# A planned decoder kernel: rotary tables first, the first head's projections moved forward, new durations and an exclusion rule in the plan

## The chip, the core and the metric

The kernel runs on one core of one Trainium2 chip. The time is that of one execution on the device in microseconds (us). The engines are PE (TensorE, matrix products), V (VectorE, "DVE" in the profile), A (ScalarE, "ACT"), G (GpSimd, "POOL") and the queue of SyncE, "SP", which issues most loads. PE, V, A and G each work through their own instructions in program order; semaphores hold an instruction until what it reads is there. "Half clock" is TensorE at 1.2 GHz instead of 2.4 GHz, 0.50 in the profile's granted clock.

## The reference

Two decoder layers on 512 tokens of width 1024, in float32:

```python
h = rms_norm(x, attn_pre_g[l]);  proj = h @ w_in[l]
qa, ka, va, qb, kb, vb, f_logit = jnp.split(proj, split_at, axis=-1)
qa = partial_rotary(...); ka = partial_rotary(...)      # first 16 of each 64 columns
oa = diff_attention(qa, ka, va, lam)                    # 4 heads, softmax 1 - lam * softmax 2
oa = rms_norm(oa, diff_sub_g[l]) * (1.0 - lam_init)
log_f = jax.nn.log_sigmoid(f_logit + forget_bias[l])
ob = forgetting_attention(qb, kb, vb, log_f)            # 8 heads, a decay added to the logits
x = x + rms_norm(concat([oa, ob]) @ w_out[l], attn_post_g[l])
h = rms_norm(x, ffn_pre_g[l])
x = x + rms_norm((silu(h @ w_gate[l]) * (h @ w_up[l])) @ w_down[l], ffn_post_g[l])
```

The cosines and sines of the rotary step come from `positions`, 512 integers.

## The kernel before

Tokens and features lie in tiles of 128 partitions by 512 columns. Every operand of a large product is split into a high part `h` (a rounded copy made by A) and a low part `l` (the rest, a subtraction by V or G), and each product is three matmuls: high by high, high by low, low by high. A weight chunk is so loaded by SP into a raw buffer (`wr`, two of them), copied by A (`wh`) and subtracted by V or G (`wl`).

A layer has these stages. **Values of the differential heads** (`va`): four banks of PSUM, one per block of 128 tokens, 24 matmuls each in four chunks. **Attention**: for each differential head a projection of k and q (`pj_kd`, `pj_qd`, 24 matmuls each), the rotary step (V: product with `cosT`, a shuffle, product with `sinT`; G: the sum), the split into `ksd` and `qsd`; then for each of four blocks of queries the scores (`sd`), their minimum on V, the exponential on A, a reciprocal on V, a scaling on G, the combination of both softmaxes on V (`ed`), the transposes on PE (`ptd`), their split on A and V, and the product with the values (`od`), normed through a further product (`ss`). The forgetting heads (`pj_kf`, `pj_qf`, `sf`, `ptf`, `of`) get their bias `ae` from G, and after the exponential a reciprocal and a scaling of `ae` on V; their values are `vb`. **Output projection** (`o`), whose weights partly use own buffers (`wo1h`, `wo1l`), then the **FFN** (`pj_g`, `pj_u`, `d`). Layer 0 begins with the loads, the norm (`h_a`), transposes (`hp_a`) and splits of `hT`.

In the attention stages the order on every engine is written by a planner. Each step is an `Op` with an engine, a duration, what it depends on, the buffers that it takes and gives, and a key; `Plan.run` keeps a clock per engine, starts the step that can start first (the lowest key among those ready), and emits the instruction. Steps of PE with the key `FILLER` (projections, `vb`, `o`) fill PE where no score, transpose or value product is ready. The planned times vanish; the order stays, and the instructions then wait for each other by semaphores alone. What the planner takes for durations are lines such as

```python
def dV(n):
    return 68 + 1.04 * n
```

in ns for n columns (`dA`, `dG` for A and G). Layer 0's beginning is planned too (`start`, `tables`). `START` sets the order of the loads. Rotary tables: SP loads the positions as eight blocks of 16 x 32, V works out the angles (`rot`), A takes sines and cosines, and the result goes to DRAM and back into `cosT` and `sinT`. The raw value weights lie in the later `mixd` and `rawv` tiles.

Of the kernel before, what the change touches and what calls it, by code (L numbers as in the profile page):

```python
# [11 lines left out]
F32 = mybir.dt.float32  # L12
F32R = mybir.dt.float32r
# [4 lines left out]
P = 128  # L18
S = 512
# [15 lines left out]
TB = S // 16  # L35
VA_C, VA_T = 4, 1
# [7 lines left out]
C_ID, C_M, C_F, NKEEP, C_U = 0, 128, 640, 641, 641  # L44
NCONST = 1153
# [15 lines left out]
class Op:  # L61
    def __init__(self, eng, dur, fn, deps, key, take, give, lat):
        self.eng, self.dur, self.fn, self.key, self.take, self.give, self.lat = eng, dur, fn, key, take, give, lat
        self.users, self.after, self.left, self.ready, self.end = [], [], 0, 0.0, None
        for d in deps:
            d.users.append(self)
            self.left += 1


class Plan:  # L70


    def __init__(self, slots, margin):
        self.free = {k: [0.0] * n for k, n in slots.items()}
        self.margin, self.ops, self.last, self.idle = margin, [], {}, None

    def add(self, eng, dur, fn, deps=(), key=0.0, take=(), give=(), lat=0.0, order="", ready=0.0):
        o = Op(eng, dur, fn, deps, key, take, give, lat)
# [18 lines left out]
    def run(self, pin, first):  # L97
        clock = dict.fromkeys("VAGQ", 0.0)
        clock["P"] = first
        cands = {e: [o for o in self.ops if o.eng == e and not o.left] for e in clock}  # L100
        todo = len(self.ops)
        while todo:
            best = None
            for e, c in cands.items():
                opts = []
                for o in c:
                    s = self.slots_at(o)
                    if s is not None:
                        r = max(s, o.ready)
                        opts.append((max(r, clock[e]), o.key, r, o))  # L110
# [12 lines left out]
            clock[o.eng] = start + o.dur  # L123
            o.end = start + o.dur + o.lat
# [34 lines left out]
def _constants():  # L159
# [6 lines left out]
    c[:, C_M + S - P:C_M + S] = np.where(r[None, :] > r[:, None], np.float32(-BIG), np.float32(0.0))  # L166
    expo = np.arange(0, ROT, 2, dtype=np.float32) / np.float32(ROT)
    inv_freq = (np.float32(1.0) / np.power(np.float32(500000.0), expo).astype(np.float32)).astype(np.float32)
    c[:, C_F] = inv_freq[r // 16]
    return c  # L170
# [3 lines left out]
def hymba_block(ctx, tc, x_d, pos_d, apre_d, win_d, fb_d, lq1_d, lk1_d, lq2_d, lk2_d, dsg_d, wout_d, apost_d,  # L174
# [64 lines left out]
    V.memset(sinT, 0.0)  # L239
    G.memset(cosT, 1.0)  # L240
# [102 lines left out]
    for l in range(DEPTH):  # L343
        win = win_d[l]
        with ExitStack() as actx:
# [12 lines left out]
            mixed_d = ap.tile([P, NDIFF, S], F32, name=f"mixd{l}", tag="v8", bufs=5)  # L358
            if l == 0:
                raw_v = ap.tile([P, NDIFF, S], F32, name=f"rawv{l}", tag="v8", bufs=5)  # L360
# [18 lines left out]
            vd, tab = [], []  # L379
# [12 lines left out]

            def start():

                plan.free.update(g=[], v8=[0.0], qs=[], ks=[])
# [9 lines left out]
                idd = dma(con[:, :P], con_d[:, :P], P)  # L405

                def w_load(c):
                    raw = (mixed_d, raw_v)[c // 2][:, 2 * (c % 2):2 * (c % 2) + 2]
                    if c == 0:
                        dst = q_tile("wva0h"), q_tile("wva0l")  # L410
                    elif c < 3:
                        w = k_tile(f"wva{c}")
                        dst = w[:, 0], w[:, 1]
                    else:
                        dst = [wpool.tile([P, WCH], F32R, name=f"{x}_va3", tag=x).rearrange("p (a b) -> p a b", a=2)
                               for x in ("wh", "wl")]
                    hi, lo = dst
                    d = dma(raw, win[2 * c * P:(2 * c + 2) * P, VA:VA + S].rearrange("(k p) n -> p k n", p=P), 2 * S)
                    ops = []
                    for k in range(2):  # L420
                        wva[2 * c + k] = hi[:, k], lo[:, k]
                        a = add("A", dA(S), lambda k=k: A.copy(hi[:, k], raw[:, k]), [d], key=-85 + c,
                                take=["w"] if c == 3 and k == 0 else [], order="hi w" if c == 3 and k == 0 else "")
# [13 lines left out]
                zeros = sinT.bitcast(mybir.dt.bfloat16)  # L437
# [16 lines left out]
                for t in range(NT):  # L454
# [24 lines left out]
                    for z in range(2):  # L479
# [20 lines left out]
                        p = add("P", 436, tr, [v, idd], key=key, take=["ts"[z]], give=["e"])  # L500
# [3 lines left out]
                for t in range(NT):  # L504
                    for c in range(4):
                        def vas(t=t, c=c):
                            if t == NT - 1:
# [4 lines left out]
                                         key=500 + VA_C * c + VA_T * t)  # L512
                    vd_split(t, [done[t, 3]])
                for c in range(4):
                    add("P", 0, lambda: None, [done[t, c] for t in range(NT)], key=-99,
                        give=(["qs", "qs"], ["ks"], ["ks"], ["w"])[c])
                add("P", 0, lambda: None, wl[2] + wl[3], key=-99, give=["v8"])
                add("P", 0, first_va.clear, [done[t, 0] for t in range(NT)], key=-99)
                return hT[NT - 1, 1]

            def tables(last):

# [3 lines left out]
                tab_d = dpool.tile([4, 8, S], F32, name="tab_d", tag="tabd")  # L526
# [4 lines left out]
                def get(dst, src, n, **kw):  # L531
                    return add("Q", max(400, 1.43 * n), lambda: nc.sync.dma_start(dst(), src), key=1, lat=2000,
                               order="ld" + "".join(f" {k}" for k in kw.get("take", ())), **kw)

                def positions():
                    w = rbuf("rd", F32, "rot")
                    x["p"] = w[:, :TB].bitcast(I32)
                    x["a"], x["n"] = w[:, TB:2 * TB], w[:, 2 * TB:3 * TB]
                    x["t"] = w[:, 4 * TB:8 * TB].rearrange("p (x j) -> p x j", x=4)
                    blocks = pos_d[0].rearrange("(b j) -> b j", j=TB)  # L540
                    return [lambda f=f: nc.sync.dma_start(x["p"][16 * f:16 * f + 16], blocks) for f in range(8)]

                def sums():
                    x["tu"] = rbuf("rc", F32, "tu")
                    return x["tu"]
                dp = add("Q", 3000, positions, key=1, lat=2000, order="ld rd", take=["rd"])
                dc = get(lambda: con[:, P:], con_d[:, P:NKEEP], S)
                du = get(sums, con_d[:, C_U:C_U + S], S, take=["rc"])

                v = op("V", 100, lambda: V.tensor_copy(x["a"], x["p"]), [dp])  # L550
                v = op("V", 100, lambda: V.tensor_scalar_mul(x["a"], x["a"], con[:, C_F:C_F + 1]), [v, dc])
                for sc in (2.0 ** 22, 2.0 ** 11, 1.0):
                    v = op("V", 100, lambda sc=sc: V.tensor_scalar(
                        x["n"], x["a"], scalar1=1.0 / (2.0 * math.pi * sc), scalar2=MAGIC, op0=ALU.mult,
                        op1=ALU.add), [v])
                    v = op("V", 100, lambda: V.tensor_scalar(x["n"], x["n"], scalar1=-MAGIC, scalar2=1.0, op0=ALU.add,
                                                             op1=ALU.mult), [v])
                    for part in _two_pi_parts():
                        v = op("V", 110, lambda sc=sc, part=part: V.scalar_tensor_tensor(
                            x["a"], x["n"], -part * sc, x["a"], op0=ALU.mult, op1=ALU.add), [v])  # L560
                v = op("V", 100, lambda: V.tensor_scalar(x["a"], x["a"], scalar1=3.1415925, scalar2=-3.1415925,
                                                         op0=ALU.min, op1=ALU.max), [v])
                v = op("V", 110, lambda: V.scalar_tensor_tensor(x["n"], x["a"], -1.0, x["a"], op0=ALU.mult,
                                                                op1=ALU.max), [v])
                a = op("A", 1500, lambda: A.activation(x["t"][:, 3], x["a"], AF.Sin), [v] + last)
                c = [op("A", 220, lambda j=j: A.activation(x["t"][:, j], x["n"], AF.Sin, bias=halfpi, scale=-1.0), [a])
                     for j in range(2)]
                v = op("V", 100, lambda: V.tensor_scalar_mul(x["t"][:, 2], x["t"][:, 3], -1.0), [a])
                p = op("A", 1300, lambda: A.preload_act_table_set("natural_log_exp_and_others"), c)
                d = op("Q", 500, lambda: nc.sync.dma_start(tab_d.rearrange("x f (b j) -> (f b) x j", j=TB), x["t"]),  # L570
                       [v, *c], lat=2000, give=["rd"])
                rows = tab_d.rearrange("x f s -> (x f) s")
                for T, r0 in ((cosT, 0), (sinT, ROT)):
                    for m in (0, HD):
                        tab.append(op("Q", 400, lambda T=T, r0=r0, m=m: nc.sync.dma_start(
                            T[m:m + ROT], rows[r0:r0 + ROT]), [d], lat=2000))
# [48 lines left out]
            def load(src, shape, name, eng=G, dst=None, take=("w",)):  # L625
# [17 lines left out]
                def lo():  # L643
# [5 lines left out]
                                give=["wr"])  # L649
# [3 lines left out]
            def fillers(pieces, deps, take={}, give=()):  # L653
# [679 lines left out]
```

## Time and profile before

| | |
|---|---|
| three runs, median | 1262.27 us (1256.56 to 1264.68) |
| the profiled execution | 1261.95 us, its span 1260.1 us |
| PE busy | 1223.8 us (97%) |
| V, A, G busy | 633.0, 520.8, 279.6 us |

The span is what the trace covers; the execution takes 1.85 us more. A matmul's end is modelled and overlaps the next one's start, so that PE looks busy while it is refilled; its idle time is what the windows leave over, and is a lower bound of what it loses.

### The profile page before, as it was taken

Reading aid. Unit: us, or ns where it says so; the run is one execution under the profiler, and the core shown is the slowest. Engines: PE = TensorE matmul, PEld = TensorE weight load, DVE = VectorE, ACT = ScalarE, POOL = GpSimd, SP = SyncE. Lnnn points to the kernel's source line nnn. Section 1 sums busy time; section 2 is a strip of 40 time slices with the busy share of each in tenths; the row PEclk is TensorE's granted clock in tenths of the full one; section 3 lists DMA queues with packets and bytes.
Section 4 is the critical chain, followed back from the end, with each engine's and each line's share of the span. In section 5 each row is a group of like instructions: output and inputs, shape, how many; then the busy total and the mean of one; then the engine's idle time right before and its main releaser. Section 6 shows DMA issues by size and latency. Waiting matters only on the chain.

```text
span 1260.1 us, 15914 instructions
## 1 busy us (share of the span) xinstructions
PE 1223.8 (97%) x5949; PEld 1015.2 (81%) x5949; DVE 633.0 (50%) x1188; ACT 520.8 (41%) x1008; POOL 279.6 (22%) x318
## 2 busy tenths in 40 slices
PE   8999999999999999999999999999999999999998
PEld 5788877798888888888877878777988888888886
DVE  7597858563333333222556867685633333332224
ACT  5465757453222222222344647674522222222221
POOL 1555557220000000000246535671100000000001
PEclk9999999999999999999999999999999999999999
DMA  7334343404333334223413333442133333332222
GB/s 241 79 84 111 93 117 103 132 18 117 98 89 98 101 101 131 88 99 106 128 35 93 88 98 93 125 129 81 51 101 100 91 93 101 100 118 87 97 100 84
DMA packets 158717, 125.94 MB, mean 100 GB/s; under 512 B 7008, under 2 KB 134112, under 8 KB 158640
## 3 DMA queue, kind: packets, MB, share of 16 engines
q1 hardware_dynamic: 158496, 124.40, 33.3%
q8 instruction: 47, 0.77, 0.3%
q10 hardware_dynamic: 144, 0.52, 0.1%
q14 instruction: 30, 0.25, 0.1%
HBM read 114.32 MB, written 2.20 MB: 92 GB/s over the span
## 4 chain that ended last, share of the span: by engine, by line
PE 56%; issue 31%; DVE 6%; ACT 3%; POOL 2%; DMA 1%; SPq 0%; POOLq 0%; DVEq 0%; ACTq 0%
PE pj_g L204 10%; PE pj_u L204 10%; PE d L204 9%; PE o L204 4%; PE pj_kd L204 3%; PE pj_qd L204 3%; PE vb L204 3%; PE va L204 3%; PE pj_kf L204 2%; PE pj_qf L204 2%; PE sd L204 2%; PE sf L204 1%; PE ptf L209 1%; PE of L204 1%; DVE ae L1033 1%
## 5 line engine op out<-in xcount | busy, mean ns | idle before, releaser
L204 PE MATMUL pj_g<-hT_h,wh_g 128*128 128x512 f32 (+1 forms) x384 | 142.9, 372 | 0.0
L204 PE MATMUL pj_g<-hT_h,wl_g 128*128 128x512 f32 (+1 forms) x384 | 142.6, 371 | 0.0
L204 PE MATMUL pj_g<-hT_l,wh_g 128*128 128x512 f32 (+1 forms) x384 | 142.6, 371 | 0.0
L204 PE MATMUL pj_u<-hT_h,wh_u 128*128 128x512 f32 (+1 forms) x368 | 140.1, 381 | 0.0
L204 PE MATMUL pj_u<-hT_l,wh_u 128*128 128x512 f32 (+1 forms) x368 | 139.8, 380 | 0.0
L204 PE MATMUL pj_u<-hT_h,wl_u 128*128 128x512 f32 (+1 forms) x368 | 139.8, 380 | 0.0
L204 PE MATMUL d<-wh_d,hh 128*128 128x512 f32 x336 | 130.8, 389 | 0.0
L204 PE MATMUL d<-wl_d,hh 128*128 128x512 f32 x336 | 130.7, 389 | 0.0
L204 PE MATMUL d<-wh_d,hl 128*128 128x512 f32 x336 | 130.7, 389 | 0.0
L258 DVE TENSOR_TENSOR wl_u<-wr_u,wh_u 128x1024 fp32r<-128x1024 f32 x44 | 53.9, 1225 | 150.2 <-ACT wh_u L257 150.2
L258 DVE TENSOR_TENSOR wl_d<-wr_d,wh_d 128x1024 fp32r<-128x1024 f32 x42 | 51.4, 1224 | 146.9 <-ACT wh_d L257 146.5
L257 ACT CAST wh_u<-wr_u 128x1024 fp32r<-128x1024 f32 x44 | 46.3, 1052 | 157.9 <-PE pj_g L204 151.6
L257 ACT CAST wh_d<-wr_d 128x1024 fp32r<-128x1024 f32 x42 | 44.3, 1054 | 157.3 <-PE d L204 134.3
L257 ACT CAST wh_g<-wr_g 128x1024 fp32r<-128x1024 f32 x44 | 46.3, 1053 | 145.8 <-issue 124.7
L1206 DVE TENSOR_TENSOR sg<-pj_u,sg 128x512 f32<-128x512 f32 x44 | 30.4, 692 | 141.7 <-PE pj_u L204 141.7
L270 POOL TENSOR_SCALAR v_fp<-s_fp 128x1 f32<-128x1 f32 x8 | 4.0, 506 | 367.0 <-ACT junk L276 366.7
L204 PEld LDWEIGHTS pj_g<-hT_h,wl_g 128*128 128x128 f32 x384 | 72.4, 188 | 12.6
L204 PEld LDWEIGHTS pj_g<-hT_l,wh_g 128*128 128x128 f32 x384 | 72.3, 188 | 12.5
L204 PEld LDWEIGHTS pj_g<-hT_h,wh_g 128*128 128x128 f32 x384 | 72.3, 188 | 12.4
L204 PEld LDWEIGHTS pj_u<-hT_h,wh_u 128*128 128x128 f32 x368 | 69.3, 188 | 13.1
L204 PEld LDWEIGHTS pj_u<-hT_h,wl_u 128*128 128x128 f32 x368 | 69.1, 188 | 13.1
L204 PEld LDWEIGHTS pj_u<-hT_l,wh_u 128*128 128x128 f32 x368 | 69.2, 188 | 12.9
(272 smaller groups left out, 2768.8 us busy)
## 6 DMA issues: line engine op xcount, KB each, us to landing
wr_g<-in_w_gate_dram SPq DMA_DIRECT2D x44, 512.0 KB, 3.8
wr_u<-in_w_up_dram SPq DMA_DIRECT2D x44, 512.0 KB, 3.8
wr_d<-in_w_down_dram SPq DMA_DIRECT2D x44, 512.0 KB, 3.4
wr_o<-in_w_out_dram SPq DMA_DIRECT2D x16, 512.0 KB, 4.2
wr_kd<-in_w_in_dram SPq DMA_DIRECT2D x8, 512.0 KB, 4.0
wr_qd<-in_w_in_dram SPq DMA_DIRECT2D x8, 512.0 KB, 4.0
ksd<-ksd SPq DMA_DIRECT2D x16, 256.0 KB, 2.9
wr_kf<-in_w_in_dram SPq DMA_DIRECT2D x8, 512.0 KB, 3.8
```

The costliest lines, as they stand in the source:

```text
L204: ins = PE.matmul(out, a, b, start=start, stop=stop)
L209: ins = PE.transpose(out, a, idn)
L257: A.copy(hi, raw)
L258: (eng or V).tensor_sub(lo, raw, hi.bitcast(F32))
L270: G.tensor_scalar(v, s2[:, 0:1], scalar1=s2[:, 1:2], scalar2=EPS, op0=ALU.add, op1=ALU.add)
L1033: return V.tensor_scalar_mul(b["e"][:, :n], b["e"][:, :n], b["l"])
L1206: V.tensor_mul(sg, pu, sg)
```

## The change

1. The rotary tables are made at the very beginning (`rotary`): A loads its trigonometric table first, then issues the gain and then the positions, one load of 128 x 4 single integers; V works on 128 x 32; A writes sines and cosines into two tiles; PE transposes these and A copies them to `cosT` and `sinT`. The way through DRAM is gone.
2. The raw value weights go into `pt` buffers, their halves into tiles of the `v8` pool, and `mixed_d` of layer 0 is made later.
3. The value matmuls of tokens 256 to 511 get a key near that of fillers, and the first head's k and q projections of layer 0 a lower one than theirs.
4. Durations in the plan grow (`dV`, `dA`, `dG`, scores, exponentials, norms).
5. A step on V marked `port` starts in the plan only after the last such step of G, and any step of G only after the last marked one of V. This is in the planner; no instruction gets a new wait from it.

```diff
-VA_C, VA_T = 4, 1
+VA_C, VA_T, VA_EARLY = 4, 1, 2
...
+        self.port = port or eng == "G"
...
                         r = max(s, o.ready)
+                        if o.port:
+                            r = max(r, port["G" if e == "V" else "V"])
...
+            if o.port:
+                port[o.eng] = start + o.dur
...
             def dV(n):
-                return 68 + 1.04 * n
+                return 110 + 1.05 * n
             def dA(n):
-                return 60 + 0.83 * n
+                return 115 + 0.83 * n
             def dG(n):
-                return 120 + 2.15 * n
+                return 180 + 2.17 * n
...
+                tc.keep_in_program_order(A.preload_act_table_set("trig_and_small"))
                 g0 = gpool.tile([P, D], F32, name="g_apre0", tag="gain")
...
+                rotary()
...
                         done[t, c] = add("P", 1390, vas, hT[t, c // 2] + wl[c] + ([done[t, c - 1]] if c else []),
-                                         key=500 + VA_C * c + VA_T * t)
+                                         key=(500 if t < VA_EARLY else FILLER - 20) + VA_C * c + VA_T * t)
...
+            def rotary():
+                key = -95
...
+                v = op("A", 500, lambda: A.dma_start(pos, pos_d[0].rearrange("(j p) -> p j", p=P)), [], lat=3000)
+                v = op("V", 80, lambda: V.tensor_copy(pf, pos), [v])
+                v = op("V", 700, lambda: [lambda f=f, c=c: V.tensor_scalar_mul(an[:, f * NT:(f + 1) * NT], pf, c)
+                                          for f, c in enumerate(_inv_freq())], [v])
...
+                for z, dep in ((0, v2), (1, v)):
+                    a = op("A", 800, lambda z=z: [place(z, half, m) for half in range(2) for m in range(2)], [dep])
+                    def tr(z=z):
+                        x[z] = (bank_t, bank_s)[z](f"rot{z}")
+                        for j in range(NT):
+                            transpose(x[z][:, j * P:(j + 1) * P], tabs[z][:, j * P:(j + 1) * P], ident)
+                    p = op("P", 436, tr, [a, idd[0]], take=["ts"[z]])
+                    ends.append(op("A", dA(S), lambda z=z: A.copy((cosT, sinT)[z], x[z]), [p], give=["ts"[z]]))
+                add("A", 0, lambda: None, ends, key=-99, give=["rc", "rc", "rd"])
...
+                du = add("Q", 1.43 * S, sums, key=1, lat=2000, order="ld rc", take=["rc"])
...
-                last_tile[:] = fillers([(650, piece(k)) for k in range(KT)], [ready], take={0: ["g"]}, give=["w"])
+                last_tile[:] = fillers([(650, piece(k)) for k in range(KT)], [ready], take={0: ["g"]}, give=["w"],
+                                       key=FILLER - 40 if kind == "d" and l == z == 0 else FILLER)
...
-                v = add("V", dV(n), top, [o], key=n_key, give=["s"])
-                return b, add("A", 282 + 0.83 * n, expo, [v], key=n_key)
+                v = add("V", dV(n)+80, top, [o], key=n_key, give=["s"])
+                return b, add("A", 370 + 0.87 * n, expo, [v], key=n_key)
...
-                    v = add("V", 75, inv, [a], key=nk)
-                    v = add("V", 70 + 0.65 * n, norm, [v], key=nk)
+                    v = add("V", 110, inv, [a], key=nk)
+                    v = add("V", 185 + 0.5 * n, norm, [v], key=nk, port=True)
```

Marked `port` in the same way: V's weight splits, the rotary product with `sinT`, the splits of `ksd` and `qsd`, the combination `ed`, the split before `ss` and the last scaling of `mixd`.

**First place: V at the beginning of layer 0.** `xs` are the tokens, `h_a` the normed ones, `rot` the angles, `hp_a` the transposed ones. Before:

```order
L468 ISA ss_a_116 128x1
L483 SCALAR_TENSOR_TENSOR h_a_162<-xs,r_s_117,g_apre_105 128x512
L483 SCALAR_TENSOR_TENSOR h_a_153<-xs,r_s_117,g_apre_105 128x512
L424 TENSOR_TENSOR wva0l_107<-mixd_101,wva0h_106 128x512 x2
L498 TENSOR_TENSOR hT_l<-hp_a_169,hT_h 128x4x128
L498 TENSOR_TENSOR hT_l<-hp_a_179,hT_h 128x4x128
```

With the change:

```order
L482 ISA ss_a_122 128x1
L555 CAST rot_107<-rot_107 128x4
L556 TENSOR_SCALAR rot_107<-rot_107 128x4 x8
L559 TENSOR_SCALAR rot_107<-rot_107 128x32
L497 SCALAR_TENSOR_TENSOR h_a_178<-xs,r_s_123,g_apre_106 128x512
L561 TENSOR_SCALAR rot_107<-rot_107 128x32
L497 SCALAR_TENSOR_TENSOR h_a_159<-xs,r_s_123,g_apre_106 128x512
L564 SCALAR_TENSOR_TENSOR rot_107<-rot_107 128x32
L438 TENSOR_TENSOR wvl_100<-rawv_112,wvh_102 128x512
```

Ten small instructions on the positions now stand ahead of the first norm, and sixteen more between it and the last norm, where before none stood.

**Second place: PE in layer 1, first differential heads.** `sd` are scores, `ptd` transposes of combined probabilities, `od` the value product of head 0. Before:

```order
L209 MATMUL ptd_6007<-con,ed_5904 128x128 x4
L204 MATMUL sd_6015<-ksd_1_5857,qsd_1_5957 128x256 x2
L204 MATMUL sd_6018<-ksd_1_5857,qsd_1_5957 128x256 x2
L204 MATMUL pj_qd_5973<-hT_h,wh_qd_5794 128x512
L204 MATMUL pj_qd_5973<-hT_l,wh_qd_5794 128x512
```

With the change:

```order
L213 MATMUL sd_6038<-ksd_1_5909,qsd_1_5985 128x128 x2
L213 MATMUL sd_6041<-ksd_1_5909,qsd_1_5985 128x128 x2
L218 MATMUL ptd_6045<-con,ed_5911 128x128 x2
L218 MATMUL ptd_6054<-con,ed_5942 128x128 x3
L213 MATMUL sd_6063<-ksd_1_5909,qsd_1_5985 128x256 x2
L213 MATMUL sd_6067<-ksd_1_5909,qsd_1_5985 128x256 x2
L218 MATMUL ptd_6074<-con,ed_5964 128x128 x4
L218 MATMUL ptd_6090<-con,ed_6049 128x128
L213 MATMUL od_6096<-pthd_5987,vdh_5664 128x512
```

Before, nine projection matmuls of 512 columns stood between the last transposes of head 0 and its value product; now the transposes, the next head's first ones and the value product follow each other, with no filler among them.

**Third place: V near the end of layer 0's forgetting heads.** `sf` are scores, `ae` their probabilities, `lf` the sums, `wo1l` a split of output weights, `wl_g` the first split of the FFN's weights. Before:

```order
L871 ISA ae_2605,mf_2644<-sf_2629,ae_2605 128x128
L871 ISA mf_2644 128x1
L645 TENSOR_TENSOR wo1l_0_2633<-wr_o_2576,wo1h_2632 128x1024
L1030 RECIPROCAL lf_2658<-lf_2658 128x1
L871 ISA ae_2621,mf_2671<-sf_2646,ae_2621 128x256
L871 ISA mf_2671 128x1
L1033 TENSOR_SCALAR ae_2605<-ae_2605,lf_2658 128x128
```

With the change:

```order
L899 ISA ae_2600,mf_2640<-sf_2624,ae_2600 128x512
L899 ISA mf_2640 128x1
L899 ISA ae_2613,mf_2649<-sf_2628,ae_2613 128x128
L899 ISA mf_2649 128x1
L899 ISA ae_2635,mf_2661<-sf_2653,ae_2635 128x256
L899 ISA mf_2661 128x1
L1059 RECIPROCAL lf_2651<-lf_2651 128x1
L1059 RECIPROCAL lf_2659<-lf_2659 128x1
L266 TENSOR_TENSOR wl_g_3050<-wr_g_3048,wh_g_3049 128x1024
L1062 TENSOR_SCALAR ae_2600<-ae_2600,lf_2651 128x512
L1062 TENSOR_SCALAR ae_2613<-ae_2613,lf_2659 128x128
```

The split of `wo1l` now stands well ahead, with three other splits and a product between it and these rows; the FFN's first split now stands right in front of two of them, where before it came after the last scaling of the layer.

## Rows read from the trace of the kernel before

**Rows 1.** The page: the span, and one of its costliest groups (V's weight split).
```profile
span 1260.1 us, 15914 instructions
...
L258 DVE TENSOR_TENSOR wl_u<-wr_u,wh_u 128x1024 fp32r<-128x1024 f32 x44 | 53.9, 1225 | 150.2 <-ACT wh_u L257 150.2
```

**Rows 2.** Windows: stretch, length; PE, PEld, V, A, G busy; granted clock; DMA share, GB/s.
```profile
0.00:21.67 21.67, 16.35 (x78) 9.95 (x79) 13.55 (x23) 13.65 (x30) 5.62 (x16) 1.00 0.82 280
...
57.77:125.00 67.23, 62.38 (x357) 53.42 (x358) 56.34 (x143) 41.99 (x104) 34.68 (x30) 1.00 0.36 94
125.00:165.00 40.00, 38.61 (x241) 33.40 (x240) 29.28 (x86) 27.45 (x69) 20.25 (x27) 1.00 0.33 89
165.00:239.50 74.50, 69.55 (x349) 55.16 (x349) 58.72 (x150) 49.93 (x115) 48.19 (x57) 0.98 0.45 134
...
660.00:745.00 85.00, 78.12 (x413) 65.81 (x412) 63.60 (x150) 46.92 (x111) 47.27 (x35) 0.96 0.33 85
745.00:790.00 45.00, 44.65 (x269) 38.55 (x268) 32.41 (x91) 29.31 (x72) 21.73 (x29) 1.00 0.38 100
790.00:863.50 73.50, 68.50 (x345) 54.30 (x344) 58.91 (x150) 48.76 (x113) 47.35 (x57) 0.98 0.45 137
```

**Rows 3.** Chain of waits: start, length, what it went through.
```profile
21.67 16.37 PE va L204 x72
...
292.56 5.44 PE pj_g L204 x24
```

**Rows 4.** Timeline of PE: start, length, line, operation, tiles, [idle before <-releaser].
```profile
63.53 1.17 PE L204 MATMUL sd<-ksd,qsd 128*128 128x512 f32 x4
...
74.18 0.63 PE L209 MATMUL ptd<-con,ed 128*128 128x128 f32 x4
...
129.95 0.44 PE L204 MATMUL sd<-ksd,qsd 128*128 128x128 f32 x2 [0.53 <-DVE qsd L705]
...
213.14 0.47 PE L204 MATMUL o<-wh_o,hT_h 128*128 128x512 f32 x1 [0.84 <-DVE qsf L705]
...
229.48 0.44 PE L209 MATMUL ptf<-con,ae 128*128 128x128 f32 x1 [1.88 <-DVE ae L1033]
...
230.58 0.63 PE L204 MATMUL o<-wh_o,hT_h 128*128 128x512 f32 x1
```

**Rows 5.** Timeline of V at two waits of PE.
```profile
227.10 2.23 DVE L1033 TENSOR_SCALAR ae<-ae,lf 128x128 f32<-128x128 f32 x1
...
723.94 2.34 DVE L810 SCALAR_TENSOR_TENSOR az<-lg 128x32 f32<-128x32 f32 x1
```

**Rows 6.** Timeline of G at the first of them.
```profile
226.90 2.35 POOL L645 TENSOR_TENSOR wo1l<-wr_o,wo1h 128x1024 fp32r<-128x1024 f32 x1
```

**Rows 7.** Timeline of V at the beginning: first and last norm, three steps of the angles.
```profile
8.24 1.41 DVE L483 SCALAR_TENSOR_TENSOR h_a<-xs,r_s,g_apre 128x512 f32<-128x512 f32 x2 [1.17 <-POOL r_s L391]
...
19.46 1.40 DVE L483 SCALAR_TENSOR_TENSOR h_a<-xs,r_s,g_apre 128x512 f32<-128x512 f32 x2
...
27.78 0.64 DVE L559 SCALAR_TENSOR_TENSOR rot<-rot 128x32 f32<-128x32 f32 x3
```

**Rows 8.** Timeline of A at the beginning: table load, a weight copy, two cosines.
```profile
1.15 1.28 ACT L464 ACT_TABLE_LOAD   x1 [1.15 <-PEq L1322]
...
22.31 1.06 ACT L641 CAST wh_kd<-wr_kd 128x1024 fp32r<-128x1024 f32 x1
...
32.21 0.53 ACT L566 ACTIVATE rot<-rot,halfpi 128x32 f32<-128x32 f32 x2
```

**Rows 9.** DMA issues: tiles, count, KB each, median us from issue to landing.
```profile
wr_kd<-in_w_in_dram SPq DMA_DIRECT2D x8, 512.0 KB, 4.0
...
rawv<-in_w_in_dram SPq DMA_DIRECT2D x2, 512.0 KB, 9.3
...
rot<-in_positions_dram SPq DMA_DIRECT2D x8, 2.0 KB, 5.4
...
dsg<-in_diff_sub_g_dram SPq DMA_DIRECT2D x2, 0.5 KB, 3.7
```

More of the change, by code (lines that the diff above doesn't have):

```diff
@@ L61, with __init__ @@
 class Op:
-    def __init__(self, eng, dur, fn, deps, key, take, give, lat):
+    def __init__(self, eng, dur, fn, deps, key, take, give, lat, port):
         self.eng, self.dur, self.fn, self.key, self.take, self.give, self.lat = eng, dur, fn, key, take, give, lat
+        self.port = port or eng == "G"
         self.users, self.after, self.left, self.ready, self.end = [], [], 0, 0.0, None
@@ L75, in __init__, with add @@
         self.margin, self.ops, self.last, self.idle = margin, [], {}, None
-    def add(self, eng, dur, fn, deps=(), key=0.0, take=(), give=(), lat=0.0, order="", ready=0.0):
-        o = Op(eng, dur, fn, deps, key, take, give, lat)
+    def add(self, eng, dur, fn, deps=(), key=0.0, take=(), give=(), lat=0.0, order="", ready=0.0, port=False):
+        o = Op(eng, dur, fn, deps, key, take, give, lat, port)
         o.ready = ready
@@ L99, in run @@
         clock["P"] = first
+        port = {"V": 0.0, "G": 0.0}
         cands = {e: [o for o in self.ops if o.eng == e and not o.left] for e in clock}
@@ L391, in rstd_ops @@
                 return r, add("G", 462, lambda: G.tensor_tensor(r, v, nhalf, op=ALU.pow), [a], key=key, lat=80)
+            idd = []
             def start():
-                plan.free.update(g=[], v8=[0.0], qs=[], ks=[])
+                plan.free.update(g=[], v8=[], rc=[], rd=[], pt=[])
+                tc.keep_in_program_order(A.preload_act_table_set("trig_and_small"))
                 g0 = gpool.tile([P, D], F32, name="g_apre0", tag="gain")
@@ L422, in w_load @@
                         a = add("A", dA(S), lambda k=k: A.copy(hi[:, k], raw[:, k]), [d], key=-85 + c,
-                                take=["w"] if c == 3 and k == 0 else [], order="hi w" if c == 3 and k == 0 else "")
+                                take=["w"] if c == 2 and k == 0 else [], order="hi w" if c == 2 and k == 0 else "")
                         ops += [a, add("V", dV(S) + 80, lambda k=k: V.tensor_sub(
@@ L499, in start @@
                         v = add("V", 663, norm, [rd, gd], key=key, take=["e"] if SQ[z] == "A" else [])
-                        p = add("P", 436, tr, [v, idd], key=key, take=["ts"[z]], give=["e"])
+                        p = add("P", 436, tr, [v, idd[0]], key=key, take=["ts"[z]], give=["e"])
                         a = add("A", dA(S), hi, [p], key=key)
@@ L517, in start, with mix @@
-                add("P", 0, lambda: None, wl[2] + wl[3], key=-99, give=["v8"])
+                def mix():
+                    nonlocal mixed_d
+                    mixed_d = ap.tile([P, NDIFF, S], F32, name=f"mixd{l}", tag="v8", bufs=5)
+                add("P", 0, lambda: None, sum(wl.values(), []), key=-99, give=["pt", "pt"])
+                half, full = ([done[t, c] for t in range(NT)] for c in (1, 3))
+                add("P", 0, lambda: None, half, key=-99, give=["v8", "v8"])
+                add("P", 0, lambda: None, full, key=-99, give=["v8", "w"])
@@ L525, in tables @@
                 x = {}
-                tab_d = dpool.tile([4, 8, S], F32, name="tab_d", tag="tabd")
                 def op(eng, dur, fn, deps, **kw):
                     return add(eng, dur, fn, deps, key=key, **kw)
[L531 to L541, printed above, removed]
@@ L552, in tables @@
[L552 to L560, printed above, removed]
@@ L561, in tables @@
[L561 to L576, printed above, removed]
+                    return nc.sync.dma_start(x["tu"], con_d[:, C_U:C_U + S])
@@ L577, in tables @@
+                tab.append(add("Q", 1.43 * S, lambda: nc.sync.dma_start(con[:, P:], con_d[:, P:NKEEP]), key=1, lat=2000,
+                               order="ld"))
+                du = add("Q", 1.43 * S, sums, key=1, lat=2000, order="ld rc", take=["rc"])
+                p = op("A", 1300, lambda: A.preload_act_table_set("natural_log_exp_and_others"), last + tab)
                 tab.append(p)
@@ L648, in load, with fillers @@
                 return box, add("G" if eng is G else "V", dG(n) if eng is G else dV(n), lo, [a], key=URGENT,
-                                give=["wr"])
+                                give=["wr"], port=True)
             last_fill, last_tile = [], []
-            def fillers(pieces, deps, take={}, give=()):
+            def fillers(pieces, deps, take={}, give=(), key=FILLER):
                 ends = []
                 for z, (dur, fn) in enumerate(pieces):
-                    o = add("P", dur, fn, (deps if z == 0 else []) + last_fill, key=FILLER,
+                    o = add("P", dur, fn, (deps if z == 0 else []) + last_fill, key=key,
                             take=take.get(z, ()), give=give if z + 1 == len(pieces) else ())
@@ L715, in stack @@
                         d = dV(S) if eng == "V" else dG(S)
-                        e = add(eng, d, lo(m), [a], key=key, give=give if m else [])
+                        e = add(eng, d, lo(m), [a], key=key, give=give if m else [], port=kind == "d")
                         if which == "k":
@@ L989, in diff_head @@
                 a2 = add("A", dA(S), sh, [a], key=key)
-                c = add("A", dA(S), lambda: A.copy(mixed_d[:, h], b["po"]), [p], key=key + 0.5, give=["t"])
-                v = add("V", dV(S), sl, [a2], key=key)
+                c = add("A", dA(S), lambda: A.copy(mixed_d[:, h], b["po"]), [p] + mix_op,
+                        key=key + 0.5, give=["t"])
+                v = add("V", dV(S), sl, [a2], key=key, port=True)
                 p = add("P", 431, ss, [v], key=key + LAG_SS, take=["s"])
@@ L998, in diff_head @@
                     mixed_d[:, h], mixed_d[:, h], dsg[:, l:l + 1], b["nrm"], op0=ALU.mult, op1=ALU.mult), [a, c],
-                    key=key + LAG_SS, give=["e"])]
+                    key=key + LAG_SS, give=["e"], port=True)]
             def fox_head(hh, n0):
```

89 lines of the change are left out of this document (54 added, 35 removed).

## The prediction

> **What bounds the kernel now.** I read the chain of waits first, then windows, then the timelines of PE, V and G around PE's longest waits. The chain shows PE's pace: 24 matmuls of 512 columns in 5.44 us, or 227 ns each [rows 3]. PE is the bound and the FFN runs at that pace; the change leaves its matmuls alone. Time can be won only where PE stands or runs slowly: at the start and in the two attention stages.
>
> The windows give the size of it. PE's idle time, length less busy, is 4.85, 1.39 and 4.95 us in three windows of layer 0 and 6.88, 0.35 and 5.00 in three of layer 1: together 23.4 us [rows 2]. Three of them ran below the full clock: 0.98 of 74.5 us, 0.96 of 85 and 0.98 of 73.5 leave out 1.5 + 3.4 + 1.5 = 6.4 us [rows 2]. PE's timeline shows where this comes from: behind a wait of 1.88 us the matmul at 230.58 lies 0.63 us long, nearly three of the steady 0.227 [rows 3, 4]. So a long wait is paid twice, once as idle time and once as a stretch at the lower of the two clock levels.
>
> What ended that wait was V's scaling of `ae`. A scaling of 128 columns lay 2.23 us on V, from 227.10, while G split a weight from 226.90 for 2.35 us [rows 5, 6]. In layer 1 a product of 32 columns, `az`, took 2.34 us [rows 5]. A whole split of 1024 columns on V is 1.225 us [rows 1]. So such a V step stands still until G's ends, which the old plan does not know. The Trainium skill, page "SBUF — State Buffer", section "SBUF: two separate sides", calls the port pair of V and G an exclusive lock for the whole instruction, held by whichever starts first; the two rows just named agree. That rule also covers V operations with both inputs in SBUF, such as `az`, which the change does not mark, and it gives case C below its ground.
>
> The start is bound elsewhere. PE's gapless run of 72 value matmuls begins at 21.67 [rows 3]. Before it V is busy 13.55 of 21.67 us [rows 2], nearly all of it between its first norm at 8.24 and the end of its last at 20.86 [rows 7]. So V sets that moment.
>
> **The change part by part.** The sum is made against the profiled execution, 1261.95 us (span 1260.1 and 1.85 around it), 0.3 below the median of the runs.
>
> 1. *Tables at the start: +4.3, between +1 and +10.* Ten small V steps now stand ahead of the first norm and wait for the positions. A issues that load behind its table load, which ends at 1.15 + 1.28 = 2.43 [rows 8], and behind the gain, so at about 2.9. No row shows this load. The nearest ones land 3.7 us after issue (128 pieces of 4 bytes) and 5.4 (the old loads of positions, which met no crowd); 9.3 is what the weights in the start's crowd take [rows 9]. I take 6.3, nearer to 5.4 than to the crowd: landing at 9.2. Three dependent steps take 0.64 us on V [rows 7], 0.21 each; the ten are smaller or equal, at half that 1.1 us. The first norm then starts at 10.3, 2.1 late. Sixteen more steps lie between it and the last norm: from nothing (in V's gaps) to 16 x 0.21 = 3.4, of which I take 1.9, since some V steps there wait for A or G anyway; one weight split of 512 columns leaves the stretch, half of 1.225 [rows 1], -0.6. The last norm ends at 20.86 + 2.1 + 1.9 - 0.6 = 24.2. A's eight sines and cosines, 0.27 each [rows 8], lie beside that. On PE the tables' transposes come first, in order, and the last `hp_a` ends near 27.3 in place of 21.67: +5.6. Six more value matmuls are done by then, 6 x 0.227 = 1.36 [rows 3]. That leaves +4.3. The low end, +1, has the load land in 3.7 and the small steps in gaps; the high end, +10, is a landing after 9.3 us with all steps at 0.21.
>
>    Next in line are the first k weights. SP issues `tu` ahead of them, and `tu` takes the buffer of the cosines, free after their transposes, near 25.5. The weights issue near 26.4, land 4.0 us later [rows 9], need A's copy of 1.06 [rows 8] and V's split of 1.2 [rows 1], and are ready near 33. PE has thirty matmuls of values after 27.3 and comes to them at 34.1: hidden by 1.1 us. If that cover is gone, each us late costs a us. The eight position loads that SP loses are far smaller and save nothing on PE. The first head's projections, now ahead of values of tokens 256 to 511, are the same matmuls in another place: nothing by themselves.
>
> 2. *Idle time in attention: -21.2.* Order alone tells how much PE work lies between a step's inputs and its use. Counted at 227 ns per 512 columns, PE's work between a block's last score and the transposes of the result averages 6.0 us before and 8.3 with the change; it grows in 81 of 96 blocks. The first head's q to its first score grows from 8.9 to 13.6 us in layer 0. V's and G's delays of about 2 us [rows 5, 6] fit into that. What stays: the wait of 0.53 for the fourth head's q at 129.95, whose distance does not grow (9.5 to 9.2), and 0.84 at 213.14 in each layer [rows 4], in sum 2.2. So 23.4 - 2.2 goes.
>
> 3. *Half clock: -6.4.* The low-clock stretches follow waits of 1.4 us and more; without those they go too [rows 2].
>
> 4. *Layer 1's cluster (second place): +5, between +3 and +8.* In layer 0 the corresponding transposes at 74.18 came 74.18 - (63.53 + 1.17) = 9.5 us after the scores [rows 4]. With the change block 512 of head 0 has 6.2 us there, and head 1's first block 1.5, where head 0's value product stands right behind. The missing 3.3 us and a wait of 1.7 or so behind it, half clock included, make 5.
>
> 5. *The FFN's first split ahead of `ae` (third place): +2, between 0 and 5.* V may stand before `wl_g` for A's copy, and then splits 1.225 us [rows 1], with PE's last transposes of the heads behind it. Twice, about 1 each.
>
> 6. *Waits in places that I can't see: +4.2, between 0 and 10,* a fifth of what term 2 takes away, since steps of both engines remain unmarked and the planned times vanish.
>
> Sum: +4.3 - 21.2 - 6.4 + 5 + 2 + 4.2 = -12.1, or **1250**.
>
> **The rivals.** *B, everything clears:* no unplaced waits, term 4 at its low end, half of term 5, and the start at +1: 1 - 21.2 - 6.4 + 3 + 1 = -22.6, **1239**. For it: the longer distances nearly everywhere. Against it: 15 of 96 blocks have less than before. On the start the Trainium skill, page "DMA: Bandwidth & Descriptors", section "Queues, rings and completion order", says that a DMA engine goes round between its queues packet by packet; by that the positions would pass the crowd and the start would cost +1 to +2 and the sum be near 1247. No run before shows it.
>
> *C, the waits come back elsewhere:* the plan's times vanish, so the exclusion is kept in the plan and not on the chip. A V step that slips by a us meets G's next one after all, and `az` and others are unmarked. If half of terms 2 and 3 comes back (13.8), the sum is +1.7 off -12.1: **1263.7**; with a quarter back (6.9) 1256.8. I put this case at **1259**. For it: the row of `az` [rows 5]. Against it: PE work ahead of the transposes has grown by 2.3 us, which is as long as one such collision.
>
> *D, slower:* the positions land late. V, behind it PE (the tables' transposes) and SP (`tu` ahead of the first weights) wait in order, so each us after 9.2 costs a us at the end. It eats the 12 us at a landing near 21 and reaches +1% near 34. The load has 512 pieces of 4 bytes, four times the 128 of the row with 3.7 us [rows 9]; four times 3.7 is 15, a landing at 18, and with the crowd's 9.3 on top 27: **1268**. Against it: a load of 512 KB in longer pieces takes 4.0 as well [rows 9], so little of the 3.7 need be the pieces.
>
> *E, nothing happens:* the new order moves work that was covered anyway, 1262. The orders differ at nearly all blocks, and PE's idle time lies there, so this is unlikely.
>
> **How the numbers follow.** Forecast 0.50, B 0.18, C 0.22, D 0.07, E 0.03. The forecast's own range is 1244 to 1256 (terms 1 and 6 by half of their bounds). Leaving out the far half of B and most of D, the range is **1238 to 1265**. About 1%, 12.6 us, is what a measurement can tell from no change here; the three runs spread over 8. Faster than 1249.6 are B and a little over half of the forecast: 0.18 + 0.27 = 0.45. Within 1% are the rest of the forecast, C, E and some of D: 0.48. Slower by over 1%: most of D and a tail of C, 0.07.
>
> **What would show it.** Start: V's cast of the positions (its idle time ends with their landing) and the first norm, 10.3 against 8.24; the gapless run of values near 27.3 against 21.67; no wait of PE at `pj_kd`. Attention: PE's idle time in the six stretches, near 10 in place of 23.4; the clock at 1.00 where 0.98 and 0.96 stood; no wait of over 1.4 us outside the cluster of layer 1, and a wait at it. End of the heads: `wl_g` on V ahead of the scalings of `ae`, and whether PE's transposes wait behind. I am wrong if V's short steps still last 2 us and PE waits for them (C), or if the positions land after 15 us (D).

## The result and the profile after

The changed kernel takes 1275.94 us, the kernel before in the same session 1261.02 (medians of four runs each): 1.0113 of before, interval 1.0090 to 1.0135. It is slower by 1.1%, where 1250 was forecast and the range ended at 1265. The profiled execution took 1275.92 us, 14.0 more than that of before.

The windows of [rows 2] on the changed kernel (length; PE, PEld, V, A, G busy; granted clock; DMA share, GB/s):

```profile
57.77:125.00 67.23, 64.42 (x367) 54.90 (x366) 52.84 (x142) 41.31 (x102) 37.44 (x30) 1.00 0.35 89
125.00:165.00 40.00, 39.62 (x247) 34.88 (x247) 29.16 (x85) 27.96 (x71) 22.12 (x28) 1.00 0.42 106
165.00:239.50 74.50, 67.27 (x337) 53.82 (x336) 55.37 (x149) 48.14 (x114) 46.36 (x56) 0.95 0.41 130
660.00:745.00 85.00, 80.07 (x410) 65.92 (x408) 57.18 (x135) 42.35 (x97) 47.48 (x34) 0.98 0.36 94
745.00:790.00 45.00, 45.00 (x276) 39.98 (x276) 34.03 (x98) 31.05 (x77) 24.82 (x33) 1.00 0.40 107
790.00:863.50 73.50, 66.41 (x336) 53.09 (x335) 55.36 (x147) 49.51 (x117) 49.36 (x57) 0.95 0.43 130
```

PE's idle time in them is 2.81 + 0.38 + 7.23 + 4.93 + 0 + 7.09 = 22.4 us; before it was 23.4. It left the stages of the differential heads (4.85 to 2.81, 6.88 to 4.93) and came back in those of the forgetting heads (4.95 to 7.23, 5.00 to 7.09), where the clock fell from 0.98 to 0.95. By this count attention has gained next to nothing, and that leaves 14 us to explain.

Most of them are in the FFN, which I took as untouched: from the first matmul of `pj_g` to the first of `d` each layer takes 248.2 us in place of 242.1. The chain of waits of the changed kernel (start, length, what it went through), for gate and up and then for down:

```profile
289.24 5.59 PE pj_u L213 x24
...
518.83 111.56 PE d L213 x492
```

24 matmuls of 512 columns take 5.59 us, 233 ns each, in place of 5.44 [rows 3] or 227. The 492 of `d` take 111.56, still 227. The granted clock is 1.00 there. A window in gate and up, where no engine waits for another, counts it; before:

```profile
300.00:400.00 100.00, 100.00 (x443) 82.84 (x442) 33.85 (x37) 28.29 (x36) 0.00 (x0) 1.00 0.33 96
```

and with the change:

```profile
300.00:400.00 100.00, 100.00 (x430) 80.31 (x429) 33.68 (x36) 28.36 (x36) 0.00 (x0) 1.00 0.32 92
```

In 100 us PE gets through 430 matmuls in place of 443. Measured between the starts of consecutive matmuls, over the whole execution, differences of at most 15 ns to the usual distance of their size (227 ns for 512 columns) add up to 20.3 us, before to 2.9. That is 17.4 us of slower pace. All larger gaps, waits and stretches at half clock together, fell from 58.1 to 53.4.

What distinguishes `pj_u` from `d`? Not an instruction: both are the same kind of matmul. It is two lines of the diff that the extract ahead of the prediction does not show:

```diff
-C_ID, C_M, C_F, NKEEP, C_U = 0, 128, 640, 641, 641
+C_ID, C_M, NKEEP, C_U = 0, 128, 640, 640
```

The rotary step's frequencies are no longer kept, so the tile of constants `con` is 640 columns wide in place of 641. Tiles lie one behind the other in SBUF in steps of 32 bytes. `hT_h` and `hT_l` stand ahead of `con` and stay; all weights and the FFN's tiles stand behind it and start 32 bytes earlier in each partition. `pj_g`, `pj_u` and the heads' projections multiply one operand from either side of `con`; both operands of `d` have moved together.

### The profile page after: what moved, and what is told of

It reads as the page before. It is cut to its first block, busy times and chain, and to the rows that moved or that the text cites. A ratio compares the mean times of both kernels' runs of the same rounds, so it can differ in the third digit from the quotient of the medians.

```text
span 1274.1 us, 15919 instructions
## 1 busy us (share of the span) xinstructions
PE 1239.6 (97%) x5958; PEld 1016.8 (80%) x5958; DVE 624.4 (49%) x1194; ACT 519.7 (41%) x1014; POOL 283.1 (22%) x319
## 4 chain that ended last, share of the span: by engine, by line
PE 62%; issue 30%; DVE 5%; ACT 2%; POOL 1%; DMA 0%; POOLq 0%; DVEq 0%; SPq 0%; ACTq 0%
PE pj_g L213 10%; PE pj_u L213 10%; PE d L213 9%; PE o L213 5%; PE pj_kf L213 4%; PE pj_qf L213 3%; PE pj_qd L213 3%; PE va L213 3%; PE vb L213 3%; PE pj_kd L213 3%; PE of L213 2%; PE ptf L218 2%; PE sf L213 1%; PE sd L213 1%; PE od L213 1%
```

## The experiments

Ratios are to the kernel before in the same session, with their intervals. "Distance" is the start of the weights' tiles less that of `hT`, modulo 256 bytes: 0 before, 224 (32 short of 256) with the change.

**e1: the weights back at their addresses.**

```diff
-con = cpool.tile([P, NKEEP], F32, name="con")
+con = cpool.tile([P, NKEEP + 1], F32, name="con")[:, :NKEEP]
```

> The changed kernel with one column put back into the constants' tile, so that every tile behind it starts 32 bytes later, where it started before the change (weights at a multiple of 64 bytes, like hT). No instruction moves. Theory S (start addresses): a matmul whose two operands start 32 bytes apart modulo 64 takes 233.5 ns per 512 columns, one whose operands agree 227; so pj_g and pj_u go back to 227 ns and the time falls by the 17.4 us that PE's small excesses add up to (20.3 less 2.9): 1258 (1254 to 1262). Rival T (the pace is that of the new order or of the chip on that day): pace stays at 233 to 234, time 1276.

1259.44 us, 0.9997 of before (0.9980 to 1.0013). The same window as above:

```profile
300.00:400.00 100.00, 100.00 (x443) 82.81 (x442) 33.85 (x37) 28.33 (x36) 0.00 (x0) 1.00 0.33 97
```

The pace is back at 443 with no instruction moved, and 16.5 us with it (small differences 3.8 us in place of 20.3). The slower result comes from these 32 bytes.

**e2: the kernel before, its weights shifted.** The tile of constants is `NKEEP + 8` wide there: distance 32.

> The kernel before with eight idle columns in the constants' tile: the weights' tiles and the FFN's start 32 bytes later, hT stays; order and instructions are those of before. Theory S: pj_g and pj_u at 233 to 234 ns, d still at 227, time 1262 + 17 = 1279 (1274 to 1284). Rival T: 227 ns everywhere, time 1262.

1275.43 us, 1.0130 (1.0101 to 1.0159), in the window:

```profile
300.00:400.00 100.00, 100.00 (x430) 80.57 (x429) 33.73 (x36) 28.39 (x36) 0.00 (x0) 1.00 0.32 93
```

The kernel before turns as slow as the changed one by eight idle columns. Theory T is refuted from both sides. I had put the time 4 us too high.

**e3 and h2: is it the distance, or the start of one operand?** Both begin with `cpool.tile([P, 8], F32, name="gap")` ahead of all tiles. e3 has the column of e1 as well, so `hT` and weights both move by 32; in h2 `hT` alone stands off a multiple of 64.

> As e1, with 32 idle bytes ahead of all tiles as well: hT and weights both start at 32 modulo 64. Theory S (only the difference of the two operands counts): 227 ns, time as e1, 1258. Rival A (each operand has to start at a multiple of 64 by itself): pj_g, pj_u and d all at 233 to 234 ns, time above 1276.

> The changed kernel with 32 idle bytes ahead of all tiles: weights and the FFN's tiles now start at a multiple of 64, hT 32 behind one, the mirror of the changed kernel. Theory S (the distance counts): pj_g and pj_u at 233 to 234 ns, d at 227, time 1275. Rival W (the weights have to start at a multiple of 64): 227 ns everywhere, 1259.

One execution each: e3 1259.08 us, h2 1275.06. The distance counts; rivals A and W fall.

**e4, g4 and h1: which distances are harmless?** `NKEEP + 17`, `+ 33` and `+ 65` columns; in h1 an unused tile behind the weights is 64 columns narrower, so that the other tiles stay.

> The changed kernel with 17 columns put into the constants' tile: weights start 64 bytes behind a multiple of 128, hT at a multiple of 128. Theory S with 64 bytes as the unit: 227 ns, time 1258 as e1. Rival B (the unit is 128 bytes or more): 233 to 234 ns, time 1276.

> The changed kernel with weights starting 128 bytes later than in e1 modulo 256. Theory B1 (the unit of the start addresses is 128 bytes): 227 ns for pj_u, time as e1, 1259. Rival B2 (the unit is 256 bytes or more): 231 to 236 ns, 1273 to 1276.

> The changed kernel with the weights' tiles 256 bytes behind their place in e1; the FFN's and the attention's tiles stand as in e1. Theory U (the unit of the start addresses is 256 bytes): pj_g and pj_u at 227 ns, time 1259 as e1. Rival (the unit is 512 bytes or more, or single distances are good and bad): 229 to 238 ns, 1272 to 1276.

One execution each; the count is of PE's matmuls from 300 to 400 us, and the times of the changed kernel, e1 and e2 are medians:

| kernel | distance | matmuls | us |
|---|---|---|---|
| before, e1, e3 | 0 | 443 | 1261.95, 1259.44, 1259.08 |
| changed, h2 | 224 | 430 | 1275.94, 1275.06 |
| e2 | 32 | 430 | 1275.43 |
| e4 | 64 | 431 | 1273.08 |
| g4 | 128 | 430 | 1275.25 |
| h1 | 0, weights 256 bytes later | 443 | 1259.77 |

My units of 64 and 128 bytes were wrong: both distances cost. A shift by 256 bytes costs nothing (theory U).

All kernels below have the addresses of e1, so that they show what the rest of the change does.

**f1, f2, g2: rule and durations.** f1 leaves out the planner's two lines `if o.port:` / `r = max(r, port[...])`; f2 has the old durations (`return 68 + 1.04 * n` and the others of the diff); g2 has both undone.

> The changed kernel with the weights' tiles at their old addresses (as e1), and the planner's exclusion rule off; the longer durations stay. Theory C (the rule acts on planned times alone; on the chip V and G meet as often as without it): time as e1, 1259 within 5, V's time beyond the shortest of each kind stays near 38 us. Rival R (the rule does keep V and G apart and covers a loss elsewhere): V's excess rises to 45 us or more and the time to 1264 to 1272.

> As e1, with the old durations in the plan and the rule on. Theory D (the longer distances between scores and transposes come from the longer durations, and they are what removed the waits of layer 0's differential heads): the waits of 1.4 to 1.7 us ahead of sd come back, time 1264 to 1270. Rival (the durations move nothing that matters): 1259 within 4.

> As e1 with the rule off and the old durations: what is left of the change is the start (tables, values, the first head's projections). With e1, f1 and f2 it makes the four corners of rule and durations. Theory P (start worth nothing, plan worth nothing by the change's own durations, the rule alone worth 0.5%): 1.000 of before (0.996 to 1.004). Rival Q (the start costs the 4.3 us of the prediction's first term and the plan as a whole hides it): 1.003 to 1.008.

| | old durations | longer durations |
|---|---|---|
| rule off | g2 1.0034 (1.0014 to 1.0055) | f1 0.9981 (0.9967 to 0.9995) |
| rule on | f2 0.9947 (0.9925 to 0.9969) | e1 0.9997 (0.9980 to 1.0013) |

Against g2 each helps alone; both together do no more than the durations alone, and less than the rule alone. V's time beyond the shortest of each kind of step, in the profiled executions, is 45.2 us before, 47.2 in g2, 55.6 in f1, 39.2 in f2 and 37.9 in e1: the rule does keep V and G apart more often (against theory C, by that number), yet time did not follow (against R). Theory D is refuted: without the longer durations the kernel is faster, and between 45 and 125 us, where PE waited 1.46, 0.31 and 1.72 us ahead of `sd` before, its longest wait ahead of `sd` in f2 is 0.28. g2 lies between P and Q and does not tell them apart.

**f3 and f4: marks where the longest wait is.** With the change PE's timeline (start, length, line, operation, tiles, [idle before <-releaser]) has one wait that is longer than any before, and its twin in layer 1:

```profile
211.44 0.51 PE L213 MATMUL sf<-ksf,qsf 128*128 128x384 f32 x2
217.86 1.30 PE L218 MATMUL ptf<-con,ae 128*128 128x128 f32 x5 [5.91 <-DVE ae L1062]
```

V's timeline in front of it:

```profile
210.68 2.87 DVE L1096 TENSOR_TENSOR hT_l<-mixf,hT_h 128x512 fp32r<-128x512 f32 x1
...
214.55 0.68 DVE L1096 TENSOR_TENSOR hT_l<-mixf,hT_h 128x512 fp32r<-128x512 f32 x1
215.16 3.45 DVE L1062 TENSOR_SCALAR ae<-ae,lf 128x512 f32<-128x512 f32 x3
```

and G's:

```profile
210.33 2.68 POOL L673 TENSOR_TENSOR wo1l<-wr_o,wo1h 128x1024 fp32r<-128x1024 f32 x1 [0.32 <-ACT wo1h L669]
...
214.65 2.79 POOL L673 TENSOR_TENSOR wl_o<-wr_o,wh_o 128x1024 fp32r<-128x1024 f32 x1
```

The same split of `hT_l` takes V 0.68 us where it starts 0.1 us ahead of G's split, and 2.87 where it starts 0.35 behind one; there it ends half a us after G. It carries no mark, so the plan saw no conflict. V is 2 us late by then, and the marked scaling of `ae`, planned clear of G, stands still until G's next split ends at 217.44. The Trainium skill, page "SBUF — State Buffer", section "SBUF: two separate sides", says that of a V operation with both inputs in SBUF and a G operation that reads SBUF the later one waits for the whole of the earlier; the row of 2.87 us agrees. f3 marks this split (`port=True` in `conv`), f4 the V steps of the forget gate's chain too (`port=eng == "V"`).

> As e1, with the V split of mixf into hT_l also marked for the rule. Theory C1 (PE's wait of 5.9 us in each layer is this split of 2.87 us on V, in place of 0.68, and behind it a scaling of ae of 2.6, each held while G splits a weight): both waits go, with their stretch at half clock, 2 x 6.1 and a little more: 1259.4 - 13 = 1246 (1244 to 1251). Rival C2 (with slips of a few us the collision only moves): 1254 to 1262.

> As f3, with the V steps of the forget gate's chain (az, ln) marked as well. Theory C1: at most 2 us below f3, since ln took 1.56 us too long once and az no longer holds PE. Rival C2: unchanged or up to 4 us slower, as every mark moves the rest of the order.

f3 took 1255.39 us, 0.9944 (0.9924 to 0.9965). PE's wait there fell from 5.91 to two of 2.39 and 1.62:

```profile
212.24 0.67 PE L218 MATMUL ptf<-con,ae 128*128 128x128 f32 x4 [2.39 <-DVE ae L1062]
214.53 0.45 PE L218 MATMUL ptf<-con,ae 128*128 128x128 f32 x1 [1.62 <-DVE ae L1062]
```

V has no slow split ahead of them now, but its scalings meet G's next one after all:

```profile
210.55 4.09 DVE L1062 TENSOR_SCALAR ae<-ae,lf 128x512 f32<-128x512 f32 x3
```

with G on

```profile
211.83 2.47 POOL L673 TENSOR_TENSOR wl_o<-wr_o,wh_o 128x1024 fp32r<-128x1024 f32 x1
```

So the unmarked split was a cause, as C1 said, but of 1.9 of the 5.91 us; the rest now comes from a collision between two marked steps, which is C2's, and 1255.39 lies in C2's range. f4 took 1251.41 us, 0.9917 (0.9899 to 0.9935), the fastest kernel here by its median: 4.0 below f3, where C1 had at most 2 and C2 nothing. In the profiled executions PE's idle time in the six windows is 15.0 us against f3's 17.5, and the clock shares leave out 3.0 against 10.8. Which of the marked steps did it was not tested.

**g1: f4 with the old durations.**

> Both gains together: weights at their old addresses, the rule with the further marks (as f4), and the old durations (as f2). Theory M (the marks act whatever the durations are): f2 and f4 add up, 0.9947 x 0.9917 = 0.9865 of before, about 1244. Rival (every new order has its own waits, so that gains do not add): 0.992 to 0.997 of before.

1253.39 us, 0.9929 (0.9908 to 0.9951): not better than f4, with intervals that overlap. The gains don't add, as the rival said.

**g3: the values and the first head as before.** `VA_EARLY` is 4, and the first head's projections have the fillers' key.

> As e1, with all value products at their old key and the first head's projections at the fillers' key. Theory P (moving the first head ahead only swaps the same matmuls and gives its rotary step more cover): PE waits ahead of the first head's scores near 59 us again, as before the change (1.5 + 0.3 us), time 1259.4 + 2, 1.001 to 1.004 of before. Rival (the head's place decides the order of all heads behind it): a change of more than 0.5% either way.

1263.16 us, 1.0013 (1.0001 to 1.0026). The size is that of theory P, its reason is not: PE does not wait ahead of the first head's scores. It waits later, in the cluster that the prediction saw in layer 1 alone (term 4) and that now stands in layer 0 too:

```profile
80.94 0.63 PE L218 MATMUL ptd<-con,ed 128*128 128x128 f32 x4 [0.86 <-DVE ed L982]
82.98 0.30 PE L218 MATMUL ptd<-con,ed 128*128 128x128 f32 x1 [1.41 <-DVE ed L982]
83.45 0.57 PE L213 MATMUL od<-pthd,vdh 128*128 128x512 f32 x1 [0.17 <-DVE ptld L947]
```

So the two moves together keep that cluster out of layer 0. The intervals of e1 and g3 overlap; what this is worth in time can't be told.

## Why the prediction failed, by its own steps

**The pace (what bounds the kernel).** "The change leaves its matmuls alone" was the step that failed. 227 ns was taken as a property of the matmul, and it belongs to matmul and addresses: +17.4 us that stand in no term, 12.2 of them in `pj_g` and `pj_u`. e1 and e2 show it in both directions. No row of before could have given the price, but the narrower tile was in the diff, and listing where tiles start was possible.

**Terms 2, 3 and 6, -21.2, -6.4 and +4.2: a third of the gain came.** The six windows hold terms 4 and 5 as well, so what they show stands against the sum of terms 2 to 6, -16.4. By the windows it is +1.7: idle time fell by 1.0, and the clock shares now leave out 3.7 + 1.7 + 3.7 = 9.1 us in place of 6.4. That is too bad a figure, because idle time in the windows is only a lower bound of what PE loses. At the usual pace (e1) the same matmuls of layer 1, from the first of `pj_kd` to the first of `pj_g`, take 231.5 us in place of 234.4; in layer 0 the first of `pj_g` starts at 267.91, before at 267.87, although the start costs 2.8. The heads gained near 2.9 us in each layer: 5.7 of the 16.4.

Term 2's reason fails. The waits ahead of the scores in the first differential heads are gone, but not by the longer distances: counted from the order as in term 2, PE's work between scores and transposes in layer 0's differential heads averages 6.8 us before, 9.2 in e1 and 6.6 in f2, and in f2 these waits are gone too. Term 3 read too much into one row: the waits of 1.46 and 1.72 us at 59.21 and 83.05 lie in a window whose clock is 1.00 [rows 2], so not every long wait was paid twice. What I overlooked is that the waits follow each other: a step that V loses to G delays all behind it, and one such pair in front of PE at 217.86 costs 5.91 us, more than PE's whole idle time in that window before (4.95). That is rival C's mechanism, to which I gave 0.22. Its size fits as well: 10.7 us came back, between C's quarter (6.9) and half (13.8), and without the pace the kernel is at 1259.4, where C stood.

**Term 1, the start: +4.3 forecast, about +2.8 measured, the near size in part by luck.** The load's issue on A's queue, then V at the beginning (as [rows 7]):

```profile
1.17 0.45 ACTq L554 DMA_DIRECT2D rot<-in_positions_dram  x1
...
6.79 0.17 DVE L555 CAST rot<-rot 128x4 f32<-128x4 int32 x1
6.99 0.67 DVE L556 TENSOR_SCALAR rot<-rot 128x4 f32<-128x4 f32 x8
7.69 0.18 DVE L559 TENSOR_SCALAR rot<-rot 128x32 f32<-128x32 f32 x1
8.12 0.75 DVE L497 SCALAR_TENSOR_TENSOR h_a<-xs,r_s,g_apre 128x512 f32<-128x512 f32 x1 [0.25 <-POOL r_s L401]
...
21.89 0.74 DVE L497 SCALAR_TENSOR_TENSOR h_a<-xs,r_s,g_apre 128x512 f32<-128x512 f32 x1
```

The positions were there by 6.79, in place of my 9.2, and the first norm waited for G and not for them: rival D is out. Of these 2.4 us 1.7 are the issue, at 1.17 in place of 2.9, so A's table load did not hold it up. From there to the landing it is at most 5.6 us, where I had 6.3. The old position loads, with 5.4 taken as meeting no crowd, had met it: they were issued from 7.33 us on, and the DMA share before was 1.03 from 9 to 15. The rule on the round of the queues, Trainium skill, page "DMA: Bandwidth & Descriptors", section "Queues, rings and completion order", asked for an early landing; this one load agrees with it and does not show it. The first norm starts at 8.12 in place of 10.3, and the last ends at 22.6 in place of 24.2. The chain then reads

```profile
25.64 6.99 PE va L213 x30
32.63 5.59 PE pj_kd L213 x24
...
43.82 8.40 PE va L213 x36
```

The first projection starts at 32.63 with 36 value matmuls still to come. Before it started at 38.04, where the 72 of [rows 3] ended; less 36 x 0.227 that is 29.87, so the start costs 2.8, its slower matmuls included. A stretch at half clock, which no term has, is part of it:

```profile
9.00:15.00 6.00, 6.00 (x19) 4.12 (x20) 5.42 (x15) 5.73 (x15) 0.89 (x2) 0.50 1.04 406
```

f3 has the same order and e1's addresses at the start, and ran this stretch at full clock:

```profile
9.00:15.00 6.00, 5.03 (x27) 3.02 (x27) 6.00 (x17) 5.75 (x16) 1.25 (x3) 1.00 1.04 405
```

V is busy throughout there, as the prediction had it, and `pj_kd` starts at 31.74, in e1 (at half clock) at 32.67. So 0.9 us of the 2.8 belong to the clock of these executions, and why it fell in them is open; V's part is about 1.9.

The first k weights were hidden, as forecast: PE goes from the values to `pj_kd` with no gap.

**Term 4, the cluster of layer 1: right.** The two sets of transposes and the value product wait one after the other:

```profile
708.17 0.63 PE L218 MATMUL ptd<-con,ed 128*128 128x128 f32 x4 [0.87 <-DVE ed L982]
710.21 0.30 PE L218 MATMUL ptd<-con,ed 128*128 128x128 f32 x1 [1.41 <-DVE ed L982]
710.68 0.47 PE L213 MATMUL od<-pthd,vdh 128*128 128x512 f32 x1 [0.17 <-DVE ptld L947]
```

and then, in a window of the form of [rows 2],

```profile
711.30:714.70 3.40, 3.40 (x14) 3.29 (x13) 0.75 (x5) 1.65 (x6) 1.28 (x1) 0.51 0.00 0
```

The waits are 2.5 us, and behind them the clock is at half for 3.4 us, half of which is lost: 4.2 in place of 5.

**Term 5, the FFN's split ahead of `ae`: 0.5 in place of 1 per layer.** It ran from 230.94 without a wait for A, and PE waited once:

```profile
232.89 0.94 PE L218 MATMUL ptf<-con,ae 128*128 128x128 f32 x5 [0.48 <-DVE ae L1062]
```

**The range**, 1238 to 1265, had room for the attention as it came out, which at the usual pace gives 1259, and none for the pace, which put 16.5 on top.

## What to carry to other kernels

When a change alters the size of any tile, list where the tiles behind it start, and compare the steady matmuls' spacing before looking for waits: here 32 bytes cost 1.3%, more than any reordering here won (f4, 0.8%). Of the distances between the two operands' starts that were tried here, 0 and 256 bytes were harmless and 32, 64, 128 and 224 cost; so time a kernel with and without a padding column before blaming its schedule. A planner's exclusion holds on the chip only as far as its times do: an unmarked step delayed the marked ones into the next collision, and with that step marked two marked ones still met.

## What the hardware showed that I had not expected

Matmuls of 512 columns ran at 227 ns with operands 0 or 256 bytes apart, at 233 (single ones 231 to 235) with 32, at 231 or 236 with 64, and at 229 or 238 with 128, in the regular part of the FFN. Those of 256 columns went the other way: 120 ns at distance 0, 117 at 224, 113 at 64. In the output projection, half of the matmuls with the weights `wo1l` have a tile that lies 128 bytes from `hT` modulo 256 even in e1, by the addresses in the built program, and most of these took 234 ns there. But of those with `wo1h`, at distance 0, 20 of 52 took 235 or 236 too; so the distance modulo 256 is not the whole of it, and why these addresses matter to PE stays open.
